# Nearest-neighbour upsampling by two on one core: the first two loads cut at row 144 instead of row 32

## The chip, the core and the metric

The kernel runs on one core of a Trainium2 chip. The engines that matter are VectorE (DVE) and ScalarE (ACT), which copy within the core's on-chip memory, SyncE (SP), which issues most transfers, and the 16 DMA engines that carry data between the chip's main memory and the on-chip memory. On-chip memory has 128 partitions. The metric is the device time of one launch in microseconds (us); a kernel's time is the median over its runs.

## The reference

```python
batch, channels, h, w = x.shape
new_h, new_w = (h * scale_factor, w * scale_factor)
...
        src_i = i // scale_factor
        src_j = j // scale_factor
        result[:, :, i, j] = x[:, :, src_i, src_j].copy()
```

The input x is float32 of shape (16, 64, 64, 64) and scale_factor is 2. Each input element becomes a block of two by two equal elements. The input has 16.78 MB, the output 67.11 MB. Nothing is computed; every byte is only moved and repeated.

## The kernel before

The input is read as 65,536 rows of 64 numbers. Each of the 128 partitions takes R = 512 consecutive rows, 128 KB that lie in one piece in main memory. An input row of 256 bytes becomes two output rows of 512 bytes, so 1 KB of output.

On-chip memory holds one large tile, `mem`. Its rear part, the view `xt`, has room for all 512 rows of a partition; in front of it lies a free region of 79 rows' worth of output (`FREE`, `WF`).

**Loads.** The list `cuts` (L192 to L193) divides the 512 rows into three loads, issued one after the other by SP at L195: rows 0 to 31, 32 to 287 and 288 to 511. Each load moves, for each partition, one run of bytes. The function `begin_before_barrier` moves these three issues ahead of the barrier that opens the program, so that they are the first thing SP does.

**Tiles.** A loop at L204 runs over nine tiles of 54, 38, 54, 61, 54, 63, 63, 63 and 62 rows. For each tile, DVE writes the expanded output of the first part of the rows (L213) and ACT that of the rest (L214); then one store (L216) sends the tile to main memory. In the first tile DVE takes 53 rows and ACT one; in the others DVE takes about five eighths, rounded down to an even number. Stores are issued by SP, but those of the tiles with n = 3 and n = 5 by ACT, which has a queue of its own.

**Where the tiles lie.** Even tiles (n = 0, 2, ...) write at the front of `mem`. Odd tiles are placed so that they end just where their own input rows begin; they overwrite input rows that earlier tiles have used up. So there are two regions that take turns. Tile 2 must wait until the store of tile 0 has landed, tile 3 until that of tile 1, and so on. Tile 1 also overwrites the input rows of tile 0, and so waits for the copies of tile 0.

**Waits on loads.** A copy waits for every load that holds a row it reads. Tile 0 reads rows 0 to 53, tile 1 rows 54 to 91, tile 2 rows 92 to 145, tile 3 rows 146 to 206, tile 4 rows 207 to 260, and tile 5 rows 261 to 323.

**Order on the queues.** On SP stand the three loads and then the stores of tiles 0, 1, 2, 4, 6, 7 and 8 in that order; each store instruction waits on SP for the tile's two copies. The function `close_early` orders the end of the program: the last store's landing is waited for by SP alone.

Of the kernel before, what the change touches and what calls it, by code (L numbers as in the profile page):

```python
# [153 lines left out]
@with_exitstack  # L154
def kernel(
    ctx: ExitStack,
    tc: tile.TileContext,
    x: bass.AP,
    scale_factor: int,
    out: bass.AP,  # L160
):
    nc = tc.nc
    nc.at_finalize(begin_before_barrier)
    nc.at_finalize(close_early)
    P = nc.NUM_PARTITIONS
    s = int(scale_factor)
    B, C, H, W = x.shape
    R = B * C * H // P
    fdt = x.dtype

    xp = x.rearrange("b c h w -> (b c h) w").rearrange("(p r) w -> p r w", p=P)
    op = out.rearrange("b c (h hd) w -> (b c h) (hd w)", hd=s).rearrange(
        "(p r) w -> p r w", p=P
    )

    rows = [54, 38, 54, 61, 54, 63, 63, 63, 62]
    GROW = s * s
    FREE = 79
    WF = FREE * GROW * W
    assert sum(rows) == R
    mem_pool = ctx.enter_context(tc.tile_pool(name="mem", bufs=1))
    mem = mem_pool.tile([P, WF + R * W], fdt, name="mem")
    xt = mem[:, WF:].rearrange("p (r w) -> p r w", r=R)

    HEAD = 32  # L192
    cuts = [0, HEAD, R // 2 + HEAD, R]  # L193
    for lo, hi in zip(cuts, cuts[1:]):
        nc.sync.dma_start(out=xt[:, lo:hi], in_=xp[:, lo:hi])  # L195

    def expanded(r0, r1):
        return (
            xt[:, r0:r1].unsqueeze(2).unsqueeze(4).to_broadcast([P, r1 - r0, s, W, s])
        )  # L200

    r0 = 0
    before = (0, 0)
    for n, k in enumerate(rows):  # L204
        size = k * GROW * W
        at = 0 if n % 2 == 0 else WF + r0 * W - size
        assert at >= before[1] or at + size <= before[0]
        before = (at, at + size)
        u = mem[:, at : at + size].rearrange(
            "p (k a w b) -> p k a w b", k=k, a=s, w=W  # L210
        )
        kv = k - 1 if n == 0 else k * 5 // 8 & ~1
        nc.vector.tensor_copy(out=u[:, :kv], in_=expanded(r0, r0 + kv))  # L213
        nc.scalar.copy(out=u[:, kv:], in_=expanded(r0 + kv, r0 + k))  # L214
        issuer = nc.scalar if n in (3, 5) else nc.sync
        issuer.dma_start(out=op[:, r0 : r0 + k, :], in_=u)  # L216
        r0 += k
# [35 lines left out]
```

## Time and profile before

| What | Before |
|---|---|
| median of three runs | 197.63 us |
| the runs | 197.63, 197.87, 197.22 us |
| span of the profiled execution (first to last instruction) | 195.7 us |
| DMA packets | 1728, of these 192 under 512 bytes |
| mean rate | 429 GB/s |
| first load: rows, size, issue to landing | 32, 1024 KB, 4.7 us |
| second load | 256, 8192 KB (256 rows of 256 bytes in 128 partitions), 23.6 us |
| third load | 224, 7168 KB, 40.2 us |
| first copy on DVE: start, length | 24.11 us, 14.3 us |
| first store: issue, landing | 38.48 us, 57.44 us |
| last store: issue | 163.4 us |

The time of a run is longer than the span, since it holds what lies before the first and after the last recorded instruction. The span is cut into 40 slices of 4.9 us in the page's row of DMA shares; a digit is the busy share in tenths, and 9 stands for 90% or more. A DMA packet here is one partition's run of bytes of one transfer; 192 small ones are those that signal a landing. A transfer's time to landing counts from its issue, so it includes what it waits for behind earlier transfers of its queue.

### The profile page before, as it was taken

How to read it: one execution, taken by the hardware profiler on the slowest of the kernel's cores; microseconds unless marked ns; L12 is line 12 of the kernel's file. 1: busy time of each engine (PE TensorE's matmuls, PEld its weight loads, DVE VectorE, ACT ScalarE, POOL GpSimd, SP SyncE). 2: the span in 40 equal slices, each digit the busy share in tenths (PEclk: the TensorE clock that was granted, in tenths of full speed). 3: DMA queues.
4: the chain of work that ended last, by engine and by line, in shares of the span. 5: the costliest groups of instructions: out<-in, count | busy, mean ns of one | idle time of the engine just before them, and what ended most of it. 6: DMA issues, size and time to landing. Idle time of an engine off the chain costs nothing.

```text
span 195.7 us, 102 instructions
## 1 busy us (share of the span) xinstructions
DVE 52.3 (27%) x9; ACT 42.1 (21%) x10; POOL 0.2 (0%) x4
## 2 busy tenths in 40 slices
DVE  0000099940026081000627200055540063000000
ACT  2000000150029700000694000059700073000000
POOL 0000000000000000000000000000000000000000
DMA  9999989889898989989999899999999999999994
GB/s 429 429 429 429 402 375 562 375 362 542 362 435 382 540 384 441 490 385 406 408 476 475 362 482 488 416 422 422 422 422 422 422 422 422 435 499 493 428 441 208
DMA packets 1728, 83.89 MB, mean 429 GB/s; under 512 B 192, under 2 KB 192, under 8 KB 192
## 3 DMA queue, kind: packets, MB, share of 16 engines
q1 hardware_dynamic: 1440, 67.63, 80.1%
q10 hardware_dynamic: 288, 16.25, 19.2%
HBM read 16.78 MB, written 67.11 MB: 429 GB/s over the span
## 4 chain that ended last, share of the span: by engine, by line
DMA 65%; ACT 11%; DVE 7%; SPq 0%; issue 0%; DVEq 0%; ACTq 0%
DMA out_dram<-mem 53%; DMA mem<-in_x_dram 12%; ACT mem L214 11%; DVE mem L213 7%; SPq L195 0%; DVEq L213 0%; ACTq L214 0%; SPq L216 0%
## 5 line engine op out<-in xcount | busy, mean ns | idle before, releaser
L213 DVE COPY mem<-mem 128x9728 f32<-128x9728 f32 (+3 forms) x9 | 52.3, 5818 | 111.0 <-DMA out_dram<-mem 86.9
L214 ACT COPY mem<-mem 128x6400 f32<-128x6400 f32 (+5 forms) x9 | 40.8, 4530 | 119.6 <-DMA out_dram<-mem 84.4
L214 ACT ACT_TABLE_LOAD x1 | 1.3, 1283 | 1.7 <-PEq L234 1.7
L234 POOL MEMSET const-bfloat16-1.0<- 128x1 bf16 x1 | 0.1, 101 | 0.0
L234 POOL MEMSET const-uint8-127<- 128x1 uint8 x1 | 0.1, 101 | 0.0
L234 POOL MEMSET const-float32-0.0<- 128x1 f32 x1 | 0.1, 98 | 0.2 <-issue 0.2
L234 POOL MEMSET const-float32-1.0<- 128x1 f32 x1 | 0.1, 98 | 0.0
## 6 DMA issues: line engine op xcount, KB each, us to landing
out_dram<-mem SPq DMA_DIRECT2D x3, 6912.0 KB, 30.1
out_dram<-mem SPq DMA_DIRECT2D x2, 8064.0 KB, 27.8
out_dram<-mem ACTq DMA_DIRECT2D x1, 8064.0 KB, 29.9
out_dram<-mem SPq DMA_DIRECT2D x1, 7936.0 KB, 32.3
out_dram<-mem ACTq DMA_DIRECT2D x1, 7808.0 KB, 29.3
mem<-in_x_dram SPq DMA_DIRECT2D x1, 7168.0 KB, 40.2
out_dram<-mem SPq DMA_DIRECT2D x1, 4864.0 KB, 26.8
mem<-in_x_dram SPq DMA_DIRECT2D x1, 1024.0 KB, 4.7
```

What stands on the lines that cost most here:

```text
L213: nc.vector.tensor_copy(out=u[:, :kv], in_=expanded(r0, r0 + kv))
L214: nc.scalar.copy(out=u[:, kv:], in_=expanded(r0 + kv, r0 + k))
L234: nc = _bacc.Bacc("TRN2", target_bir_lowering=False, num_devices=1)
```

## The change

The first cut moves from row 32 to row 144. The first two loads then have 144 rows each; the second cut, row 288, and the third load remain. Everything else remains as it is: the tiles, the engines that copy, the queues, the order of issue.

```diff
-    HEAD = 32
-    cuts = [0, HEAD, R // 2 + HEAD, R]
+    MORE = 288
+    cuts = [0, MORE // 2, MORE, R]
     for lo, hi in zip(cuts, cuts[1:]):
         nc.sync.dma_start(out=xt[:, lo:hi], in_=xp[:, lo:hi])
```

In `cuts`, [0, 32, 288, 512] becomes [0, 144, 288, 512]. The loads have 1024, 8192 and 7168 KB before, and 4608, 4608 and 7168 KB after. Tile 0 reads rows of the first two loads before, and of the first alone after; so does tile 1 after, which before reads only rows of the second. Tile 2 reads rows of the second load before, and after the change rows 92 to 143 from the first and rows 144 and 145 from the second.

## The prediction

> **What bounds the kernel now.** I read the page first (busy shares, DMA row, queues), then stretches of the span, then the chain of waits, the issues of transfers with their landing times, and the order of time. Behind these I used the trace's records of single DMA packets (start, duration, bytes), from which I rebuilt what each of the 16 DMA engines did one packet after another.
>
> The page, shares of the span and the queues:
>
> ```profile
> DVE 52.3 (27%) x9; ACT 42.1 (21%) x10; POOL 0.2 (0%) x4
> ...
> q1 hardware_dynamic: 1440, 67.63, 80.1%
> q10 hardware_dynamic: 288, 16.25, 19.2%
> HBM read 16.78 MB, written 67.11 MB: 429 GB/s over the span
> ```
>
> The two compute engines work a quarter of the time. The two queues' packets fill 80.1 + 19.2 = 99.3% of 16 engines' time. Whatever isn't packets is 0.7% of 195.7, some 1.4 us an engine.
>
> Long stretches of the span (columns: stretch, length, busy DVE, ACT, POOL, clock, share of the 16 DMA engines, GB/s):
>
> ```profile
> 1.00:24.00 23.00, 0.00 (x0) 1.28 (x1) 0.00 (x0) 1.00 1.06 450
> 24.00:38.48 14.48, 14.37 (x2) 0.41 (x2) 0.00 (x0) 1.00 1.03 444
> 38.48:57.44 18.96, 2.91 (x1) 3.60 (x1) 0.00 (x0) 1.00 0.94 406
> 57.44:130.00 72.56, 19.73 (x5) 20.86 (x5) 0.00 (x0) 1.00 1.01 436
> 130.00:163.40 33.40, 15.26 (x3) 15.90 (x3) 0.00 (x0) 1.00 1.00 433
> ```
>
> A packet is booked whole where it starts, so short stretches swing around 1.00; no stretch shows an empty DMA. The packet records say it sharper. From its first packet (1.01 to 1.37 us, by engine) to its last (ending at 194.8 to 195.4) each engine has the next packet begin as the last one ends. Loads and stores go at one pace: 65,536 bytes every 2.414 us, 55,296 every 2.038, which is 27.1 bytes per ns. The 96 packets of one engine (12 transfers of 8 partitions, 5,242,880 bytes) make 193.2 us at these steady intervals; the records hold another 0.3 to 0.8 us of packets that took longer than their like. So 1.4 + 193.2 + 0.7 is the 195.4 at which the last packet ends.
>
> The chain of waits (start, length, what), its first third:
>
> ```profile
> 0.43 23.58 DMA mem<-in_x_dram
> ...
> 24.11 14.30 DVE mem L213
> ...
> 38.48 18.96 DMA out_dram<-mem
> ...
> 57.47 4.89 ACT mem L214
> ...
> 62.38 32.09 DMA out_dram<-mem
> ```
>
> It reads as if load, copy and store took turns. They don't: while the copy of 24.11 to 38.41 runs, the third load is moving, and the store issued at 38.48 has 18.96 us to landing, though its 6912 KB need 8 x 2.038 = 16.3 at the steady interval. It queued behind the third load:
>
> ```profile
> mem<-in_x_dram SPq DMA_DIRECT2D x1, 7168.0 KB, 40.2
> ...
> mem<-in_x_dram SPq DMA_DIRECT2D x1, 1024.0 KB, 4.7
> mem<-in_x_dram SPq DMA_DIRECT2D x1, 23.6
> ```
>
> The last number is us to landing: all three loads are issued in the first 1.33 us and land one after another, in order (the third, issued at 0.90, at some 40.6). The bound is bytes through 16 engines that never run dry.
>
> **The change, part by part.**
>
> *The loads' sizes.* Three loads, 16.78 MB and 128 runs per load stay, so 96 packets an engine stay. Eight packets of 8,192 bytes (0.3055 us apart) and eight of 65,536 (2.414) become sixteen of 36,864: 36,864 / 27.15 = 1.358 us. 16 x 1.358 = 21.73 against 8 x 0.3055 + 8 x 2.414 = 21.76: a gain of 0.03 us. SP's three issue instructions take 0.381, 0.426 and 0.432 us for three very different sizes, so they cost the same again.
>
> *The cold start.* The first one to three packets of each engine took longer than the steady 0.309: extra time of 0.21 to 0.65 us an engine, the first packet taking 0.354 to 0.954, and on more than half of the engines a second or third one 0.1 to 0.5 too long. How a first packet of 36,864 bytes starts, the trace does not show. If the second stall is the wait for something that a longer first packet hides, up to 0.36 is saved on a typical engine; if the extra is a fixed latency, nothing changes; if it grows with the packet, it costs (a rival below). The stalls end by 2.5 us on nearly all engines, whichever packet they struck, which speaks for a latency. I take a gain of 0.1.
>
> *The first copy.* Rows 0 to 53 need 54 rows; before, these end inside the second load (landing 23.59), now inside the first. The first load lands at about 1.3 + 0.4 + 8 x 1.358 + 0.3 = 12.9 (0.3 is from last packet to landing of the second load). The copies at L213 (14.29 us) and L214 (0.40) start at 13 and not 24.1, and end at 27.3. The store is issued at some 27.4, not 38.48. All of this lies beside loads: the queue then holds 13 us of loads, up to 40.2, so on SP's queue the first store still starts at 40.2 and still lands at about 57. Nothing is gained but cover: store packets were ready at best 1.0 to 1.4 us after issue (the lag of the first load), 39.5 to 39.9, and the first engine ran out of loads at 40.18. That margin of 0.3 to 0.7 us becomes about 11.
>
> *The second pair of copies* (3.08 on DVE, 3.61 on ACT) moves from 38.5–42.1 to 27.4–31.0, and its store from 42.1 to 31. Nothing follows: its store starts behind the first one's 16.3 us.
>
> *Waits.* The third tile (rows 92 to 145) waits for the second load because of rows 144 and 145; that landed at 23.6, and the tile can't start before the first store lands at 57.4 anyway, since it writes the same region. Behind it on ACT and DVE stand only later tiles, which wait for later stores. The cut at row 288 stays, so every wait for the third load stays.
>
> *Loads to stores.* The last load packet of an engine (38.0 to 40.8) took up to 0.33 us longer than its like, some 0.10 on average. Two readings: the store's packets came just in time, and with them early this vanishes (a gain of 0.1 on average, 0.33 on the worst engine); or the copies of 38.48 to 42.1 slowed it. Then they will now lie under loads for all of 3.6 us instead of 1.9, and 0.10 becomes 0.19 (worst 0.33 becomes 0.63): a loss of 0.1 to 0.3. During the long copy before it packets took at most 0.04 longer, which speaks for the first reading, and during the third tile's copies (57.5 to 62.4) stores show none. I take a gain of 0.1. By the Trainium skill ("SBUF — State Buffer", section "SBUF: two separate sides") a transfer and a compute engine use separate ports and cannot slow one another; by that rule alone the loss is ruled out and the gain of 0.1 to 0.33 would stand; no row here settles it.
>
> *Sum.* 0.03 + 0.1 + 0.1 = 0.23 us off a span of 195.7: 195.5. The median of the runs, 197.63, is 1.9 above the span (start and end outside it), so 197.4.
>
> **The rivals.**
>
> A: *both doubtful terms at their good end.* 0.03 + 0.36 + 0.33 = 0.72 off: 196.9. For it: the engine that ended last (195.37) carried 0.37 cold and 0.33 at the turn. Against: then the next engine decides, at 195.34 with 0.65 cold, and its cold extra was all in its first packet.
>
> B: *the chain of waits is the bound.* The copy starts 11 us earlier and so does all behind it: 186.6. Against: 193.2 us of packets at a pace that never varied.
>
> C, slower: *the cold stretch costs by the byte.* The place is the first packet of each engine. Were its slowness a rate, an engine that took 0.676 for 0.309 would need 1.361 x 2.19 = 2.98 for 36,864 bytes: 1.62 lost where 0.37 was, 1.25 more, and as no engine ever idles later nothing catches up: 198.9. It decides from 0.59 us more, that is from a factor of 1.7 on a late engine. Against: third and later packets were at full pace at the same moments as other engines' first ones stalled.
>
> D: *the copies slow the loads:* a loss of 0.3 at the turn, none of the other gains: 197.9.
>
> That the change does nothing at all to the copies is not to be had: it would show as a first copy at 24 us.
>
> **How the numbers follow.** 0.3% of 197.63 is 0.59 us, about what a measurement of this kernel can tell from no change (its three runs span 197.22 to 197.87). Forecast (within 0.3%): 0.74. A: 0.14, on the fast side. B: 0.02. C: 0.06. D: 0.04, half of it past the bound together with noise. Faster 0.14 + 0.02 = 0.16; same 0.74 + 0.02 = 0.76; slower 0.06 + 0.02 = 0.08. The time is the forecast's, 197.4. The range goes from A's end less a tenth, 196.8, to D with a spread of the medians of 0.2, 198.1; C, B and a little of A are left out, about 0.12.
>
> **What would show it.** Right: first copies at about 13, first store issued at 27 to 28 and still landing at 56.5 to 57.5 (about 29 us after issue, not 19); the second load still landing at 23.6, the third at 40.5; DMA at 1.00 in every long stretch; the last store landing within 0.6 of 195.7. Wrong: any stretch of empty DMA; the first store landing far from 57; first-load packets at other than 1.36 us after the first; loads landing later, together with copies.

## The result: half a per cent slower, and the profile after

The changed kernel takes 198.41 us (median of six runs, 198.18 to 198.53) against 197.64 for the kernel before (six runs). The ratio is 1.0047, with a 95% interval of 1.0037 to 1.0057. The forecast was "within 0.3%" at 197.4, with a range up to 198.1. So the time lies 0.3 us above the range and the change made the kernel slower.

The page of the changed kernel, first its span, shares and queues:

```profile
span 197.1 us, 102 instructions
...
DVE 52.3 (27%) x9; ACT 42.0 (21%) x10; POOL 0.2 (0%) x4
...
q1 hardware_dynamic: 1440, 67.63, 80.1%
q10 hardware_dynamic: 288, 16.25, 19.0%
HBM read 16.78 MB, written 67.11 MB: 426 GB/s over the span
```

The same bytes, the same packets, the same work on the engines, and queues that again fill 99.1% of the 16 DMA engines' time. By this view nothing is idle, so the loss has to be looked for in the single packets.

The chain of waits of the changed kernel (start, length, what):

```profile
0.00 13.27 DMA mem<-in_x_dram
...
13.29 14.30 DVE mem L213
...
27.67 31.14 DMA out_dram<-mem
...
58.89 4.89 ACT mem L214
```

The first copy starts at 13.29 and the first store is issued at 27.67, as the prediction had them. But the third tile starts at 58.89, which was 57.47: the first store landed 1.4 us later than before, though it was issued 10.8 us earlier. The last store too lands 1.4 us later (197.08 against 195.72).

The seven microseconds around the end of the loads, 36 to 43, in 40 slices of 0.175 us, show where. A packet is booked where it starts, so each comb of digits is one round of packets on the 16 engines. First the kernel before, then the changed one:

```profile
DMA  9900000000099900000000099979000000099790
GB/s 1311 983 0 0 0 0 0 0 0 0 0 2294 1966 983 0 0 0 0 0 0 0 0 0 1264 1264 1580 316 632 0 0 0 0 0 0 0 1896 1896 316 948 0
```

```profile
DMA  9990000000009990000000000000007997770000
GB/s 655 2949 1638 0 0 0 0 0 0 0 0 0 328 2621 2294 0 0 0 0 0 0 0 0 0 0 0 0 0 0 0 316 2212 1580 316 316 316 0 0 0 0
```

The second comb (slices 12 to 14 before, 13 to 15 after, about 38.0 to 38.6 us) is the last load packet of each engine; the third is the first packet of the first store. Before, the third comb comes some 12 slices, 2.1 us, after the second, which is what a packet of 57,344 bytes takes. After, it comes some 18 slices later, 3.2 us. The packet records give it by engine: beyond the steady 2.116 us, the last load packet took 0.10 us more before (0.00 to 0.33) and 1.10 more after (0.72 to 1.52). Nothing is empty in this time: the packets themselves are longer, which is why the queues' share doesn't show it.

On average over the engines the last packet ends at 194.97 us before and 196.23 after, 1.26 later. Of this 1.00 is that one packet; 0.19 is a slower first packet and 0.09 a later first start, which may be chance (taken up below, with the cold start). The two profiled spans lie 1.4 us apart and the medians only 0.77, because the execution profiled before was a quick one: in the runs taken beside the experiments, this kernel had a span of 195.7 at 197.01 us and of 196.3 at 197.65. What lies outside the span is 1.3 us, not the 1.9 that the prediction took.

### The profile page after: what moved, and what is told of

It is laid out like the page before. It is cut to its first block, busy times and chain, and to the rows that moved or that the text cites. A ratio compares the mean times of both kernels' runs of the same rounds, so it can differ in the third digit from the quotient of the medians.

```text
span 197.1 us, 102 instructions
## 1 busy us (share of the span) xinstructions
DVE 52.3 (27%) x9; ACT 42.0 (21%) x10; POOL 0.2 (0%) x4
## 4 chain that ended last, share of the span: by engine, by line
DMA 66%; ACT 10%; DVE 7%; issue 0%; ACTq 0%; SPq 0%
DMA out_dram<-mem 59%; ACT mem L214 10%; DVE mem L213 7%; DMA mem<-in_x_dram 7%; ACTq L214 0%; SPq L216 0%
## 5 line engine op out<-in xcount | busy, mean ns | idle before, releaser
L213 DVE COPY mem<-mem 128x9728 f32<-128x9728 f32 (+3 forms) x9 | 52.3, 5817 | 112.4 <-DMA out_dram<-mem 99.1
```

## Experiments

Theory 1: the extra falls on a load packet when the store already waits behind it on its queue. The rivals were the sizes of the loads, and the copies of the second tile, which ran during the turn from loads to stores before (38.5 to 42.1) and no longer do. "Extra" is always the mean over 16 engines of what the last large load packet took beyond its steady time.

**Hold the store back in the changed kernel.** DVE copies 41 rows of the first tile ahead of the tile's own copy, which writes them again:

```diff
+        if n == 0:
+            nc.vector.tensor_copy(out=u[:, :41], in_=expanded(0, 41))
         nc.vector.tensor_copy(out=u[:, :kv], in_=expanded(r0, r0 + kv))
```

> The changed kernel, with a copy of 41 rows on DVE ahead of the first tile's copy, which writes what that copy writes again: some 11.0 us more, so that both pairs of first copies and the first store come as late as in the kernel before (store issued at some 38.7 us). Theory 1 (the last load packet of each engine is held up by 1.1 us because the first store waits behind it early): that extra falls from 1.1 to 0.1-0.2 us and the time to 197.6-197.9, ratio 1.000 to 1.0015; what stays is the slower first packet, about 0.2 us. Rival (the larger first loads themselves cause it): extra still 1.1, time 198.4, ratio 1.004.

It missed its aim. DVE worked on the second tile between the two copies of the first (the second of these had to wait for the first), so the store was issued at 41.66 and not at 38.7. The extra is 0.00 on all engines, but now the engines run dry. The stretches of this run (share of the DMA engines and GB/s at the end):

```profile
1.00:38.00 37.00, 24.71 (x3) 1.69 (x2) 0.00 (x0) 1.00 1.01 429
38.00:42.00 4.00, 3.57 (x1) 0.33 (x1) 0.00 (x0) 1.00 0.53 229
```

The share of 0.53 is a true gap: 1.8 to 2.3 us on each engine between its last load packet and its first store packet. The stores behind the gap were slower too, by 0.005 us in most packets and 0.5 us an engine in all; in the profiles of the two kernels it is 0.02 or less. 199.51 us, ratio 1.0108 (1.0092 to 1.0124). The extra vanishes with the same loads, which speaks against the load sizes; too late costs more than too early.

**Hurry the store in the kernel before.** In the first tile DVE takes 52 rows and ACT two:

```diff
-        kv = k - 1 if n == 0 else k * 5 // 8 & ~1
+        kv = k - 2 if n == 0 else k * 5 // 8 & ~1
```

> The kernel before, loads of 32, 256 and 224 rows, with 52 rows of the first tile on DVE and two on ACT; an even number of rows is copied at about twice the pace (some 7.1 us instead of 14.3), so the first store is issued at some 31.2 us and not at 38.5, the loads untouched. Theory 1 (early store): the extra of the last load packets rises from 0.1 to about 1.1 us, time 198.4-198.7, ratio 1.004 to 1.005. Rival (load sizes): extra 0.1, time 197.6, ratio 1.000.

The loads of 32, 256 and 224 rows are untouched. In order of time (start, length, engine, what):

```profile
24.29 10.09 DVE L213 COPY mem<-mem 128x13312 f32<-128x13312 f32 x2 [24.29 <-DMA mem<-in_x_dram]
...
31.47 32.48 SPq L216 DMA_DIRECT2D out_dram<-mem  x3
```

Both DVE copies together now take 10.09 us instead of 17.29, and the first store is issued at 31.47. The same seven microseconds of this run, 36 to 43:

```profile
DMA  9990000000009990000000000000009999700000
GB/s 655 3277 1311 0 0 0 0 0 0 0 0 0 655 3277 1311 0 0 0 0 0 0 0 0 0 0 0 0 0 0 0 948 1264 1264 1264 316 0 0 0 0 0
```

The third comb has moved to where the changed kernel has it. Extra 1.11 (0.65 to 1.49), 198.22 us, ratio 1.0044 (1.0031 to 1.0056). The whole loss comes back with the old load sizes and a faster copy: the sizes are not the cause.

**Copies early, store late.** Two runs in the changed kernel take the copies of the first two tiles where the change put them, and hold back both first stores by DVE copies that rewrite half of the first tile's output with what is there:

```diff
+        if n == 0:
+            u0 = u
+            r0 += k
+            continue
+        if n == 1:
+            nc.vector.tensor_copy(out=u0[:, :53, 1], in_=u0[:, :53, 0])
+            nc.vector.tensor_copy(out=u0[:, :7, 1], in_=u0[:, :7, 0])
+            nc.sync.dma_start(out=op[:, : rows[0], :], in_=u0)
```

> The changed kernel with the copies of the first two tiles as early as there (13 to 31 us), but the first two stores held back to some 38.7 us by two DVE copies that rewrite half of the first tile's output with what is there. Theory 1 (when the store is queued): extra 0.1-0.3, time 197.6-197.9, ratio 1.000 to 1.0015. Rival 2 (the copies have to run at the turn for it to be cheap; DVE at work at 38-41 us): extra near 1.1, ratio 1.004.

The rewriting ran at twice the pace that I had reckoned, so the store went out at 35.06. Extra 0.99, ratio 1.0044 (1.0032 to 1.0057): no verdict between the theories, but a further point. In the second form the 53 rows are rewritten twice and then three rows:

```diff
+            nc.vector.tensor_copy(out=u0[:, :53, 1], in_=u0[:, :53, 0])
-            nc.vector.tensor_copy(out=u0[:, :7, 1], in_=u0[:, :7, 0])
+            nc.vector.tensor_copy(out=u0[:, :3, 1], in_=u0[:, :3, 0])
```

> The changed kernel (144, 144, 224 rows) with both pairs of first copies early (13 to 31 us), and the first two stores held back by three DVE copies that rewrite half of the first tile's output with what is there: first store at some 38.6 us, second right behind it. Theory 1 (time of the store's issue alone): the extra falls to 0.0-0.3 and the ratio to 0.999-1.001. Rivals (load sizes; copies no longer at the turn): extra 1.0 and ratio 1.004.

In order of time:

```profile
27.72 3.61 ACT L214 COPY mem<-mem 128x4096 f32<-128x4096 f32 x1 [13.98 <-DVE mem L213]
...
38.64 0.35 SPq L223 DMA_DIRECT2D out_dram<-mem  x1
39.10 23.76 SPq L225 DMA_DIRECT2D out_dram<-mem  x2
57.62 4.43 DVE L213 COPY mem<-mem 128x8192 f32<-128x8192 f32 x1 [19.07 <-DMA out_dram<-mem]
```

The last copy of the second tile starts at 27.72 as in the changed kernel; only the stores are late, at 38.64 and 39.10. The combs of 36 to 43:

```profile
DMA  9997000000009999000000007999000000009990
GB/s 655 2621 1638 328 0 0 0 0 0 0 0 0 655 2621 1311 655 0 0 0 0 0 0 0 0 316 2212 1896 632 0 0 0 0 0 0 0 0 948 2528 1580 0
```

Twelve slices from comb to comb, extra 0.003 (0.00 to 0.01), 197.11 us, ratio 0.9993 (0.9983 to 1.0002). The changed loads and the early copies are as harmless as the prediction said; holding back the issue of the first two stores gave back all of the loss. A repeat follows below.

**Move the issue by halves of a microsecond in the kernel before.** With 51 rows on DVE (an odd number, so at the slow pace) the store is issued at 38.07; with 47 instead of the 51 in this line, at 37.00:

```diff
-        kv = k - 1 if n == 0 else k * 5 // 8 & ~1
+        kv = 51 if n == 0 else k * 5 // 8 & ~1
```

> The kernel before with 51 rows of the first tile on DVE and three on ACT: the first store is issued half a microsecond earlier, at some 37.9 us. Store packets are then ready at 38.9 to 39.3, still after the last load packet of each engine has begun (38.0 to 38.5). Theory 1a (the extra of some 1.0 us falls on a load packet that begins while store packets already wait behind it): extra as before, 0.0-0.3, ratio 1.000 to 1.001. Rival 1b (what counts is how long the store has waited when the loads end; a graded cost): some 0.3-0.6 extra, ratio 1.001 to 1.003.

Extra 0.33 (0.11 to 0.55), 197.39 us, ratio 1.0004 (0.9993 to 1.0015).

> The kernel before with 47 rows of the first tile on DVE and seven on ACT: first store issued at some 36.9 us, its packets ready at 37.9 to 38.3, on most engines before the last load packet begins. Theory 1a: extra near 1.0 on most engines, ratio 1.003 to 1.005. Rival 1b: 0.5-0.8, ratio 1.002 to 1.004. If the load sizes or the copies' place were the cause, extra 0.1 and ratio 1.000.

Extra 1.17 (0.83 to 1.45), 198.16 us, ratio 1.0039 (1.0023 to 1.0055). One microsecond of issue time makes nearly the whole loss. The first of the two fits neither form well: its extra lies at the edge between them. In order of time, the second:

```profile
24.23 15.69 DVE L213 COPY mem<-mem 128x12032 f32<-128x12032 f32 x2 [24.23 <-DMA mem<-in_x_dram]
37.00 3.61 ACT L214 COPY mem<-mem 128x4096 f32<-128x4096 f32 x1 [11.16 <-DVE mem L213]
37.00 26.74 SPq L216 DMA_DIRECT2D out_dram<-mem  x3
```

Both engines copy the second tile through the turn here (to 39.92 and 40.61), as in the kernel before, and the extra is there all the same. Nor is it the second store: that is issued at 40.63 here, later than the 39.10 of the run without an extra.

**A little later than before.** DVE copies of 41 numbers, into a spare place, ahead of the first tile's copy; three of them, one, and two:

```diff
+        if n == 0:
+            for j in range(3):
+                spare = mem[:, size + 42 * j : size + 42 * j + 41]
+                nc.vector.tensor_copy(out=spare, in_=mem[:, WF + 40 * W : WF + 40 * W + 41])
```

> The kernel before with three DVE copies of 41 numbers ahead of the first tile's copy, into a spare place that nothing reads: the first store some 0.3 us later, at 38.8. Its packets are ready at 39.8 to 40.2, the loads end at 40.1 to 40.5. Theory 1a: no extra at all on the last load packet; if gaps of up to 0.1 us open on a few engines, ratio 0.999 to 1.000. Rival 1c (the kernel before is already at the edge): gaps of 0.3 us, ratio 1.001 to 1.002.

Issue at 38.92: extra 0.00, gaps of 0.14 on average (0.46 at most), and the store packets that follow took 0.4 us an engine more in all than in the kernel before, as behind the gap of the first experiment. 197.59 us, ratio 1.0008 (0.9999 to 1.0017).

> The kernel before with one DVE copy of 41 numbers (into a spare place that nothing reads) ahead of the first tile's copy: first store at some 38.6 us, 0.15 later than before, as late as in the version of early copies and late store, with the old load sizes. Theory 1: no extra on the last load packets and no gap, 0.1-0.3 us better than the kernel before, ratio 0.9985 to 0.9995. Rival (it was the place of the copies or the even loads that made that version quick): ratio 1.000, extra 0.1.

The one copy was hidden: the store went out at 38.49, no later than before. Extra 0.04, ratio 0.9999 (0.9988 to 1.0009): it told nothing apart.

> The kernel before with two DVE copies of 41 numbers ahead of the first tile's copy: first store at some 38.7 us. Theory 1: between 38.48 (extra 0.04-0.09) and 38.92 (no extra, but gaps of 0.1 and slower packets behind) lies the best time; extra 0.0, gaps below 0.05, 0.1-0.2 us better than the kernel before, ratio 0.999 to 0.9997. Rival (the time just after has its own price): ratio 1.000 to 1.0008.

Issue at 38.73: extra 0.002, gaps of 0.05, ratio 1.0000 (0.9991 to 1.0009). Expected 0.999 to 0.9997; the gain did not come. Some engines had already run dry while others had not.

**Another queue.** The changed kernel with the first tile's store issued by ACT:

```diff
-        issuer = nc.scalar if n in (3, 5) else nc.sync
+        issuer = nc.scalar if n in (0, 3, 5) else nc.sync
```

> The changed kernel with the first tile's store issued by ACT at some 27.7 us, so that it does not queue behind the third load but shares the DMA engines with it. If a turn from loads to stores costs because an engine passes from the one to the other, sharing makes many turns: if each costs a part of 1.1 us over some eight packet pairs, 2 to 8 us more, ratio 1.01 to 1.04. If only the queueing behind a load in one queue costs, the 1.1 us goes: 197.6, ratio 1.000.

Load and store packets then alternate from 33 to 51 us. The load packet before the first store packet took 0.78 to 1.54 us more (1.12 on average over the 16 engines), the later load and store packets of this stretch 0.0 to 0.41, most of them under 0.25. By engine some 2.3 us more than the steady pace in all; 199.69 us (six runs from 199.51 to 202.05), ratio 1.0134 (1.0099 to 1.0169). So it isn't being behind a load in the same queue: the first passage costs about the same 1.1 us, and mixing costs on top.

**A small last load.** The changed kernel with four rows split from the third load:

```diff
-    cuts = [0, MORE // 2, MORE, R]
+    cuts = [0, MORE // 2, MORE, R - 4, R]
```

> The changed kernel with its third load cut in two, rows 288 to 507 and 508 to 511, so that the packets ahead of the waiting first store have 1,024 bytes and not 57,344. Theory 1d (the cost is a fixed time where an engine passes from loads to a store that already waits): some 1.0 us more than the steady pace is spent around the turn, whichever packets show it, ratio 1.004. Rival 1e (the cost is a share, about half, of the last load packet's own 2.1 us): it shrinks to 0.0-0.1 us and the time to 197.4-197.6, ratio 1.000 to 1.001.

The small packets took 0.046 us each and lost nothing; the large packet before them, with eight small ones between it and the store, took 1.12 more (0.79 to 1.57). So the cost is not a share of the packet next to the store; it strikes some packets ahead. 198.57 us, ratio 1.0072 (1.0059 to 1.0085). That is more than the 1.004 expected, and the eight extra packets don't explain it: eight large packets less 0.037 us each pay for nearly all of eight small ones. The profiled span is the 197.1 of the changed kernel; the kernel before was quicker beside this run (197.23) than beside the others. Why is not shown.

**The version that beats both, once more.**

> The version of early copies and late store with 144, 144 and 224 rows once more, with more rounds, for its ratio: 0.9993 before, with an interval that reached 1.0002. Theory 1: extra 0.0, 0.1-0.3 us better than the kernel before, ratio 0.9985 to 0.9995, interval below 1. Rival (no different from the kernel before): ratio 1.000.

Issue at 38.70, extra 0.005, 197.20 us against 197.42 beside it, ratio 0.9986 (0.9977 to 0.9995). It is faster than the kernel before, by little, and 1.2 us faster than the changed kernel, though it does 7.9 us of DVE work that changes nothing. By the two ratios it gains 0.14 to 0.28 us on the kernel before, so that one seems as a rule to lose a little more at its turn than the 0.10 of its one profile. This would explain why the medians of the two kernels lie 0.77 apart and not the 1.00 of the packets; it is an estimate, not shown by a profile.

The issue times on SP's queue in one table; "early" is the time from the issue to where the loads would end on average at the steady pace:

| first store issued | early by | loads | extra on the last large load packet | ratio |
|---|---|---|---|---|
| 27.67 (the change) | 12.9 | 144, 144, 224 | 1.10 | 1.0047 |
| 31.47 | 9.0 | 32, 256, 224 | 1.11 | 1.0044 |
| 35.06 | 5.5 | 144, 144, 224 | 0.99 | 1.0044 |
| 37.00 | 3.4 | 32, 256, 224 | 1.17 | 1.0039 |
| 38.07 | 2.4 | 32, 256, 224 | 0.33 | 1.0004 |
| 38.48 (before) | 1.8 | 32, 256, 224 | 0.10 | 1 |
| 38.49 | 1.8 | 32, 256, 224 | 0.04 | 0.9999 |
| 38.64 | 1.9 | 144, 144, 224 | 0.003 | 0.9993 |
| 38.70 | 1.8 | 144, 144, 224 | 0.005, gaps 0.01 | 0.9986 |
| 38.73 | 1.8 | 32, 256, 224 | 0.002, gaps 0.05 | 1.0000 |
| 38.92 | 1.6 | 32, 256, 224 | 0.00, gaps 0.14 | 1.0008 |
| 41.66 | −1.1 | 144, 144, 224 | 0.00, gaps 2.04 | 1.0108 |

At 1.8 to 1.9 the extra is anything from 0.002 to 0.10: there the mean time alone no longer tells which it will be.

## Why the prediction was wrong

*The bound* was right: packets without gaps, one pace, and copies that cost nothing where they are. *The loads' sizes* were right: packets of 36,864 bytes came 1.360 us apart (1.358 predicted), and the second load landed 23.8 us after its issue (23.6 predicted), which is 24.2 on the span's clock against 24.0 before. Two slips in the working cost nothing: 1.4 + 193.2 + 0.7 makes 195.3 and not 195.4, and the third load landed before at 41.1, not at some 40.6, since its 40.2 us count from its issue at 0.90.

*The cold start.* A gain of 0.1 was taken, and 0.19 more was measured in this pair of profiles; no run shows the gain. Of the seven profiles with a first load of 32 rows two had 0.43 and 0.47 there (one of them the profile that I had) and five 0.63 to 0.74; of the seven with 144 rows one had 0.56 and the others 0.61 to 0.73. Seen further on, the third load's packets begin on average at 23.61 to 23.65 in all seven with 144 rows, and at 23.34, 23.38 and 23.52 to 23.65 with 32. So a quick start was only ever seen with the small first load. Whether the change takes it away, at up to 0.3 us in some executions, or it is chance, seven profiles of each don't settle. The loss does not hang on it: with 144 rows and a late store nothing is lost (ratios 0.9993 and 0.9986). Rival C, a cold start by the byte, would have shown 1.6 us there; it is ruled out.

*The first copy and its store* is the step that failed. The prediction let the early store wait behind the loads at no price: "Nothing is gained but cover". It looked for the price of coming late, and there it was right in kind (an empty DMA of 2.0 us, and 1.1% in all, when the issue is 3.2 us later). It had no price for coming early. The runs show one: 1.0 to 1.2 us on each engine as soon as the store is issued some 3.4 us or more before the loads end, no matter how much earlier, and 0.10 or less at 1.8 to 1.9.

*Loads to stores.* The row was the right one to look at: last load packets that took up to 0.33 longer. Both readings of it were wrong. Store packets that came early did not remove the extra, they are its cause; the kernel before was already at the edge of it. The copies had no part: the extra is 0.003 with DVE at work until 38.55 and ACT idle, 0.99 with both idle from 35.0 on, and 1.17 with both at work from 37.0 to 39.9. The Trainium skill ("SBUF — State Buffer", section "SBUF: two separate sides") says that transfers and compute engines do not slow one another; these three runs agree. So rival D named the place, with the wrong mechanism and a third of the price. The sum was mis-sized there by 1.1 us: a gain of 0.1 was taken, a loss of 1.0 came.

The Trainium skill ("DMA: Bandwidth & Descriptors", section "Rules for kernel authors") advises, to overlap a transfer with compute, to issue it early, so that its fixed cost overlaps. Here issuing the store early costs 0.4%; the rule names no such price, and for this case the measurement decides.

What stays open is what the DMA engine does in that microsecond. That the large packet was struck with small ones between it and the store may mean that an engine looks several packets ahead, and the alternating run may mean a cost of the first store more than of each passage; neither was tried apart, and neither is shown.

## What to carry to other kernels

Where the DMA is the bound and its queue is always full, the order and the moment at which transfers are queued can still matter: a store queued long behind the last loads cost 1.1 us here, and one queued 3.2 us later than before left every engine empty for 2.0 us. Before costing an earlier issue at nothing, look at the single packets around a turn from loads to stores, and compare their durations with those of the same size elsewhere; shares of busy time don't show packets that grow. Work that looks needlessly slow (here a copy of 53 rows at half the pace of 52) may be what sets such a moment.

## What was not expected of the hardware

The 16 engines, 99% busy by their queues, lost 1.1 us each in one packet, with no gap in the records. The window in which an issue is neither too early nor too late is about half a microsecond wide: 2.4 us before the end of the loads gives an extra of 0.33, 1.8 to 1.9 us gives 0.002 to 0.10, and 1.6 us opens gaps of 0.14. And DVE's copy of 52 rows (13,312 numbers a partition) took 7.1 us where 53 rows (13,568) took 14.3.
